# Reordering the attention slot: scores and their maximum first, reciprocal and scaling one slot behind

## The chip, the cores and the metric

The kernel runs on one core of one Trainium2 chip. The metric is device time in microseconds. The engines are named as in the profile: PE is TensorE (matrix products and transposes), PEld its weight loads, DVE is VectorE, ACT is ScalarE, POOL is GpSimd and SP is SyncE, which here only issues DMAs. Each engine takes its own list of instructions from the front, and waits for the others by semaphores.

## The reference

One encoder layer on 512 tokens of width 2048, all in float32. The part that matters here is the attention: eight heads of group A (every query sees all 512 keys) and eight of group B (three dilated windows; they amount to a mask that is added to the scores, since the branches are merged by their softmax denominators).

```python
h = rmsnorm(x, g_mix)
qa, ka, va, qb, kb, vb = split(h @ w_in)
# group A: q, k normalised and rotated, 8 heads of 128, two k/v heads
sc = einsum('bqkgd,bskd->bkgqs', q, k); p = softmax(sc); o = einsum('bkgqs,bskd->bqkgd', p, v)
# group B: the same with the windows (128,1), (512,4), (2048,16), merged by their denominators
x = x + concat(rmsnorm(a), rmsnorm(b)) @ w_out
x = x + (silu(gate) * up) @ w_down          # gate, up = split(rmsnorm(x) @ w_gate_up)
return rmsnorm(x, g_final)
```

## The kernel before

Every float32 product is made from three: each operand is split into a high part (fp32r) and the rest (low part), and `mm3` (L236 to L240) multiplies high by high, high by low and low by high into one bank of PSUM. A split (`split`, L229 and L230) is an ACT copy for the high part and a DVE subtraction for the low part. Weights are split in the same way when they have been loaded (L290 on ACT, L295 on DVE).

The program is written out in the order in which each engine is to run it; no scheduler moves anything. Its main loop goes over units. A unit in the part that matters here multiplies one block of 128 weight rows with the four tiles of 128 tokens, which is twelve products of 512 columns. Ahead of a unit's products, `prepare` issues loads and weight splits of later units; behind them come tasks from a list named `side`, as many as a credit allows (`HEAD_RATE`: 1.42 per unit during the input projection of group B's q and k, 1.9 during the output projection; a slot of group A costs 1.5, one of group B 1.2). So in the input projection less than one slot falls to a unit, and in the output projection now and then two slots follow each other with no unit in between.

The slots are the attention's share of `side`. There are 16 heads of four slots each, and slot s = 4h + i issues, in `head_slot`, the work of several heads at different stages. `score(i)` makes the scores of 128 queries against 512 keys, takes their maximum on DVE (in group B together with the mask, which also moves them from PSUM to the tile p, L572; in group A only the maximum, L568), takes the exponential on ACT with the row sums (L574 and L569), and then, on DVE, the reciprocal of the sums (L576) and the scaling of p by it (L577). Six slots after a head's first scores (`TURN_LAG`), `pt(kb)` transposes the kb-th block of keys of all four p tiles on PE (L583) into one bank, and `split` makes the turned P's high part pTh (ACT) and low part pTl (DVE) from it. Eight slots after (`VALUE_LAG`), `pv(kb)` multiplies V with them. `fin` copies a head's output to the tile oT, stores it to DRAM from ACT's queue (L603), and squares it (L606 or L609) for the later norm. `tq` and `tk` transpose the q and k of a head four and two slots ahead of its first scores.

PSUM has eight banks, which `bank` takes from the front of a queue and `release` puts at its end. A projection chunk holds four of them, a running P·V product one. The tiles named by `slot` share storage that is laid out over the whole program from each tile's first to its last use.

Of the kernel before, what the change touches and what calls it, by code (L numbers as in the profile page):

```python
# [14 lines left out]
AF = mybir.ActivationFunctionType  # L15
# [8 lines left out]
NT = S // P  # L24
# [33 lines left out]
TURN_LAG = 6  # L58
VALUE_LAG = 8
# [8 lines left out]
def encoder_block(ctx, tc, x, g_mix, w_in, g_q_a, g_k_a, g_out_a, g_out_b, w_out, g_ffn,  # L68
                  w_gate_up, w_down, g_final, c_ident, c_mask, c_axial, c_partial, out):
    nc = tc.nc  # L70
# [9 lines left out]
    def nm(base):  # L80
        counter[0] += 1
        return f"{base}_{counter[0]}"

    def slot(base, dtype=F32, shape=(P, 512)):
        return sp.tile(list(shape), dtype, tag="s", name=nm(base))
# [11 lines left out]
    def bank():  # L97
        return banks.popleft()

    def release(*tiles):  # L100
        banks.extend(tiles)
# [3 lines left out]
    def small(n=4):  # L105
        used[0] += n
        assert used[0] <= 512
        return smalls[:, used[0] - n:used[0]]
# [127 lines left out]
    def mm3(dst, a, b, start, stop, chained=False):  # L236
        (ah, al), (bh, bl) = a, b
        nc.tensor.matmul(dst, ah, bh, start=start, stop=False, skip_group_check=chained)  # L238
        nc.tensor.matmul(dst, ah, bl, start=False, stop=False, skip_group_check=chained)  # L239
        nc.tensor.matmul(dst, al, bh, start=False, stop=stop, skip_group_check=chained)  # L240

    def cols(pair, lo, n=P):
        return pair[0][:, lo:lo + n], pair[1][:, lo:lo + n]
# [288 lines left out]
    class Head:  # L532
# [27 lines left out]
        def score(self, t):  # L560
            if t == 0:
                self.negm, self.z, self.rz = small(), small(), small()
            ps = bank()
            mm3(ps, cols(self.q, t * P), self.k, True, True)
            p = slot("p")
            nmx, z, rz = self.negm[:, t:t + 1], self.z[:, t:t + 1], self.rz[:, t:t + 1]
            if self.kind == "A":
                nc.vector.tensor_reduce(nmx, ps, axis=AX.X, op=OP.max, negate=True)  # L568
                nc.scalar.activation(p, ps, AF.Exp, bias=nmx, accum_out=z)  # L569
            else:  # L570
                lo = (NT - 1 - t) * P
                nc.vector.tensor_tensor_reduce(p, ps, mask[:, lo:lo + S], -1.0, 3e38, op0=OP.add, op1=OP.min,  # L572
                                               accum_out=nmx)
                nc.scalar.activation(p, p, AF.Exp, bias=nmx, scale=-1.0, accum_out=z)  # L574
            release(ps)
            nc.vector.reciprocal(rz, z)  # L576
            nc.vector.tensor_scalar(p, p, rz, None, op0=OP.mult)  # L577
            self.p[t] = p

        def pt(self, kb):  # L580
            ps = bank()
# [42 lines left out]
    def head_at(slot):  # L624
        h, i = divmod(slot, NT)
        return (heads[h], i) if 0 <= h < len(heads) else (None, i)

    def head_slot(s):
        head, i = head_at(s - TURN_LAG)
        if head:  # L630
            head.pt(i)
        head, i = head_at(s - VALUE_LAG)
        if head:
            head.pv(i)
            if i == NT - 1:
                head.fin()
        head, i = head_at(s)
        if head:
            head.score(i)
        for lead in ("tq", "tk"):  # L640
            head, i = head_at(s + {"tq": 4, "tk": 2}[lead])
            if head and i == 0:
                getattr(head, lead)()

    def weighed(cost, f):
        f.cost = cost
# [5 lines left out]
    def attention_tasks():  # L652
# [38 lines left out]
        for s in range(2 * NHA * NT + VALUE_LAG + 1):  # L691
            cost = 1.5 if s < NHA * NT else 1.2 if s < 2 * NHA * NT else 0.7
            todo += [weighed(cost, lambda s=s: head_slot(s))] + extra.get(s, [])
# [580 lines left out]
    at = [0.0]  # L1274
# [56 lines left out]
    for n, u in enumerate(units):  # L1331
# [20 lines left out]
        while side and credit >= getattr(side[0], "cost", 1.0):  # L1352
            f = side.popleft()
# [58 lines left out]
```

## Time and profile before

| what | value |
|---|---|
| median of 3 runs | 2008.81 us (2008.07 to 2009.35) |
| profiled execution | 2008.06 us, span 2006.3 us |
| granted TensorE clock, mean | 0.996 |
| PE busy | 1982.6 us, 99% |
| DVE busy | 1565.2 us, 78% |
| ACT busy | 1113.2 us, 55% |
| POOL busy | 129.1 us, 6% |

The profile gives each engine's busy time, the groups of instructions by line with the idle time ahead of them and what ended it, the waits summed by who waited for whom, the chain of work that ended last, and the timeline. The span is the time from the first to the last instruction of the profiled execution. "L583" is line 583 of the kernel; where a helper issues an instruction, its line is the helper's, so the pieces of `split` and `mm3` are told apart by the tiles that they write and read (`b` is a bank of PSUM, `smalls` a column of small per-row values, `arena` a large tile that also holds split weights and activations).

### The profile page before, as it was taken

The numbers are of one execution on the slowest core, as the hardware profiler recorded it, in microseconds if no ns is written. First come the engines' busy times: TensorE is split into PE (matmuls) and PEld (weight loads), VectorE is DVE, ScalarE is ACT, GpSimd is POOL, SyncE is SP. The second block draws the span as 40 slices with busy tenths as digits, with TensorE's granted clock in tenths as the row PEclk, the third lists the DMA queues.
The fourth block names the chain that finished last, engine by engine and source line by source line (L and its number), as shares of the span: only waits on it lengthen the run. The fifth ranks groups of instructions, "written<-read, shape, count | busy, mean of one in ns | idle before, by whom it ended". The sixth has DMA issues, their size and how long they took to land.

```text
span 2006.3 us, 27422 instructions
## 1 busy us (share of the span) xinstructions
PE 1982.6 (99%) x9019; PEld 1632.3 (81%) x9019; DVE 1565.2 (78%) x2786; ACT 1113.2 (55%) x1984; POOL 129.1 (6%) x161
## 2 busy tenths in 40 slices
PE   9999999999999999999999999999999999999997
PEld 7888888887788888888888888888888888788886
DVE  6887876666764688878877878778789887877968
ACT  8655345455544565555555555545545666666655
POOL 0000100000010000000000000000000122111121
PEclk9999999999999999999999999999999999999999
DMA  8576533335244645737647558458367698768765
GB/s 275 179 280 230 178 116 99 106 133 166 91 140 138 210 144 197 268 123 260 233 147 275 196 182 283 152 195 299 122 240 253 194 279 251 191 172 270 195 159 168
DMA packets 231135, 390.61 MB, mean 195 GB/s; under 512 B 21408, under 2 KB 70352, under 8 KB 230864
## 3 DMA queue, kind: packets, MB, share of 16 engines
q1 hardware_dynamic: 204736, 325.87, 48.2%
q0 software_dynamic: 15280, 34.09, 8.2%
q10 hardware_dynamic: 10976, 28.91, 4.1%
q8 instruction: 70, 1.15, 0.2%
q14 instruction: 73, 0.60, 0.1%
HBM read 325.08 MB, written 63.70 MB: 194 GB/s over the span
## 4 chain that ended last, share of the span: by engine, by line
PE 92%; DVE 3%; issue 2%; ACT 2%; DMA 1%; POOL 0%; ACTq 0%; POOLq 0%; DVEq 0%
PE b L238 29%; PE b L239 29%; PE b L240 29%; PE b L583 1%; DVE tw L780 1%; PE b L1084 1%; DVE raw L817 1%; DMA x<-x1d 0%; PE b L1009 0%; PE b L319 0%; PE b L545 0%; DVE pTl L230 0%; DMA oA<-oT 0%; POOL x1d L1156 0%; DMA oB<-oT 0%
## 5 line engine op out<-in xcount | busy, mean ns | idle before, releaser
L238 PE MATMUL b<-tw,arena 128*128 128x512 f32 x2136 | 837.5, 392 | 2.5 <-ACT ev L1155 2.5
L239 PE MATMUL b<-tw,arena 128*128 128x512 f32 x2136 | 831.9, 389 | 0.6 <-DVE tw L780 0.5
L240 PE MATMUL b<-tw,arena 128*128 128x512 f32 x2136 | 832.3, 390 | 0.1
L777 ACT ACTIVATE tw<-raw 128x512 fp32r<-128x512 f32 x924 | 559.1, 628 | 433.3 <-DVE raw L817 282.7
L780 DVE TENSOR_TENSOR tw<-raw,tw 128x512 fp32r<-128x512 f32 x924 | 618.7, 686 | 169.8 <-ACT tw L777 166.6
L238 PEld LDWEIGHTS b<-tw,arena 128*128 128x128 f32 x2136 | 401.0, 188 | 84.9 <-ACT ev L1155 3.6
L240 PEld LDWEIGHTS b<-tw,arena 128*128 128x128 f32 x2136 | 400.9, 188 | 84.8 <-DVE arena L330 0.5
L239 PEld LDWEIGHTS b<-tw,arena 128*128 128x128 f32 x2136 | 401.2, 188 | 83.7 <-DVE tw L780 1.8
L817 DVE TENSOR_TENSOR raw<-raw,raw 128x512 f32<-128x512 f32 x528 | 361.5, 685 | 1.1 <-DMA raw<-in_w_gate_up_dram 0.9
L238 PE MATMUL b<-w,arena 128*128 128x512 f32 x368 | 146.1, 397 | 0.0
L239 PE MATMUL b<-w,arena 128*128 128x512 f32 x368 | 143.6, 390 | 0.7 <-DVE w L295 0.7
L240 PE MATMUL b<-w,arena 128*128 128x512 f32 x368 | 143.8, 391 | 0.0
L1156 POOL DMA_DIRECT2D x1d<-ev x76 | 66.4, 974 | 1147.1 <-ACT ev L1155 1127.2
L239 PEld LDWEIGHTS b<-w,arena 128*128 128x128 f32 x368 | 69.2, 188 | 15.3 <-DVE w L295 1.5
L240 PEld LDWEIGHTS b<-w,arena 128*128 128x128 f32 x368 | 69.1, 188 | 14.9
L777 ACT ACTIVATE tw<-stage 128x512 fp32r<-128x512 f32 x96 | 58.0, 628 | 40.2 <-DVE stage L817 29.4
L238 PEld LDWEIGHTS b<-w,arena 128*128 128x128 f32 x368 | 69.1, 188 | 13.5
L780 DVE TENSOR_TENSOR tw<-stage,tw 128x512 fp32r<-128x512 f32 x96 | 64.0, 686 | 12.2 <-ACT tw L777 12.1
L295 DVE TENSOR_TENSOR w<-raw,w 128x512 fp32r<-128x512 f32 x96 | 64.8, 684 | 6.5 <-ACT w L290 3.5
L230 DVE TENSOR_TENSOR pTl<-b,pTh 128x512 fp32r<-128x512 f32 x64 | 43.9, 687 | 30.8 <-ACT pTh L229 28.1
L290 ACT ACTIVATE w<-raw 128x512 fp32r<-128x512 f32 x96 | 58.2, 622 | 15.6 <-PE b L239 6.8
L357 DVE TENSOR_TENSOR pair<-pair 128x256 f32<-128x256 f32 x120 | 45.5, 421 | 26.2 <-ACT pair L1012 25.1
(193 smaller groups left out, 1749.9 us busy)
## 6 DMA issues: line engine op xcount, KB each, us to landing
raw<-in_w_gate_up_dram SPq DMA_DIRECT2D x616, 256.0 KB, 5.3
raw<-in_w_down_dram SPq DMA_DIRECT2D x176, 256.0 KB, 6.8
stage<-in_w_in_dram SPq DMA_DIRECT2D x112, 256.0 KB, 5.3
forms<-pair SPq DMA_DIRECT2D x22, 896.0 KB, 5.3
x1d<-ev POOLq DMA_DIRECT2D x76, 256.0 KB, 6.8
fr<-forms ACTq DMA_DIRECT2D x35, 512.0 KB, 6.0
raw<-in_w_in_dram SPq DMA_DIRECT2D x64, 256.0 KB, 5.2
raw<-in_w_out_dram SPq DMA_DIRECT2D x32, 512.0 KB, 4.6
```

What stands on the lines that cost most here:

```text
L230: nc.vector.tensor_tensor(lo, src, f32(hi), op=OP.subtract)
L238: nc.tensor.matmul(dst, ah, bh, start=start, stop=False, skip_group_check=chained)
L239: nc.tensor.matmul(dst, ah, bl, start=False, stop=False, skip_group_check=chained)
L240: nc.tensor.matmul(dst, al, bh, start=False, stop=stop, skip_group_check=chained)
L290: nc.scalar.activation(self.w[0], src, AF.Copy)
L295: nc.vector.tensor_tensor(self.w[1], self.src, f32(self.w[0]), op=OP.subtract)
L357: nc.vector.tensor_tensor(out, x, y, op=op)
L583: nc.tensor.transpose(ps[:, t * P:(t + 1) * P], self.p[t][:, kb * P:(kb + 1) * P], ident)
L777: nc.scalar.activation(self.pair[:, 0], self.src, AF.Copy)
L780: nc.vector.tensor_tensor(self.pair[:, 1], self.src, f32(self.pair[:, 0]), op=OP.subtract)
L817: nc.vector.tensor_tensor(t[dst], t[src[0]], t[src[1]], op=OP.add if form == "m6" else OP.subtract)
L1156: nc.gpsimd.dma_start(x1_dram[2 * cb + j, row], e, accum_op=OP.add)
```

## The change

The exponential leaves `score` for a step of its own, `exp`, and the reciprocal with the scaling goes to `norm`. A slot issues, in this order: scores and maximum of slot s; reciprocal and scaling of the scores of slot s-1; transposes and split of P (lag 6); the exponential of slot s; P·V (lag 8) and, at a head's end, `fin`; then `tq` and `tk`. Before, the order was: transposes and split of P, P·V and `fin`, then scores, maximum, exponential, reciprocal and scaling, then `tq` and `tk`. In group A the bank with the scores is released after the exponential, which now stands behind the transposes; in group B it is released after the masked maximum, as that reads it last.

```diff
-            p = slot("p")
-            nmx, z, rz = self.negm[:, t:t + 1], self.z[:, t:t + 1], self.rz[:, t:t + 1]
+            p = self.p[t] = slot("p")
+            nmx = self.negm[:, t:t + 1]
             if self.kind == "A":
                 nc.vector.tensor_reduce(nmx, ps, axis=AX.X, op=OP.max, negate=True)
-                nc.scalar.activation(p, ps, AF.Exp, bias=nmx, accum_out=z)
+                self.raw = ps
             else:
                 lo = (NT - 1 - t) * P
                 nc.vector.tensor_tensor_reduce(p, ps, mask[:, lo:lo + S], -1.0, 3e38, op0=OP.add, op1=OP.min,
                                                accum_out=nmx)
+                release(ps)
+
+        def exp(self, t):
+            p, nmx, z = self.p[t], self.negm[:, t:t + 1], self.z[:, t:t + 1]
+            if self.kind == "A":
+                nc.scalar.activation(p, self.raw, AF.Exp, bias=nmx, accum_out=z)
+                release(self.raw)
+            else:
                 nc.scalar.activation(p, p, AF.Exp, bias=nmx, scale=-1.0, accum_out=z)
-            release(ps)
+
+        def norm(self, t):
+            p, z, rz = self.p[t], self.z[:, t:t + 1], self.rz[:, t:t + 1]
             nc.vector.reciprocal(rz, z)
             nc.vector.tensor_scalar(p, p, rz, None, op0=OP.mult)
-            self.p[t] = p
...
     def head_slot(s):
-        head, i = head_at(s - TURN_LAG)
-        if head:
-            head.pt(i)
-        head, i = head_at(s - VALUE_LAG)
-        if head:
-            head.pv(i)
-            if i == NT - 1:
-                head.fin()
-        head, i = head_at(s)
-        if head:
-            head.score(i)
-        for lead in ("tq", "tk"):
-            head, i = head_at(s + {"tq": 4, "tk": 2}[lead])
-            if head and i == 0:
-                getattr(head, lead)()
+        def at(lag, f, only=None):
+            head, i = head_at(s - lag)
+            if head and (only is None or i == only):
+                f(head, i)
+        at(0, Head.score)
+        at(1, Head.norm)
+        at(TURN_LAG, Head.pt)
+        at(0, Head.exp)
+        at(VALUE_LAG, Head.pv)
+        at(VALUE_LAG, lambda head, i: head.fin(), NT - 1)
+        at(-4, lambda head, i: head.tq(), 0)
+        at(-2, lambda head, i: head.tk(), 0)
```

## The prediction

> **What bounds the kernel now.** I read the page first, then busy time by stretches of the span, then the waits inside the stretch with holes, then the timeline of the largest hole. The head of the page:
>
> ```profile
> span 2006.3 us, 27422 instructions
> PE 1982.6 (99%) x9019; PEld 1632.3 (81%) x9019; DVE 1565.2 (78%) x2786; ACT 1113.2 (55%) x1984; POOL 129.1 (6%) x161
> ```
>
> TensorE is the bound, and it stands idle for only 2006.3 - 1982.6 = 23.7 us. The edit keeps all instructions, so it can win only TensorE's idle time in the attention, and time lost to a lowered clock. Busy time by stretches (time, then busy us of each engine and instruction count, granted clock, DMA), and below them the transposes of P (shortest, median, longest in ns, first and last start), which say where the slots lie:
>
> ```profile
> 240.00:440.00 200.00, 199.97 (x970) 164.72 (x969) 134.96 (x316) 98.09 (x208) 13.24 (x12) 1.00 0.33 106
> 440.00:545.00 105.00, 96.22 (x465) 76.86 (x464) 74.18 (x179) 57.45 (x121) 6.24 (x5) 0.97 0.43 140
> 545.00:590.00 45.00, 45.00 (x225) 36.98 (x224) 29.21 (x59) 24.04 (x48) 6.59 (x5) 1.00 0.43 142
> 474.64:480.43 5.79, 2.90 (x16) 1.82 (x14) 3.76 (x9) 2.91 (x6) 0.00 (x0) 0.92 0.85 291
> 480.43:486.59 6.16, 6.16 (x17) 5.03 (x18) 4.26 (x11) 3.90 (x9) 0.00 (x0) 0.52 0.20 66
> ...
> L583 PE MATMUL b<-fixed,p x256: 270/272/475, 272.4 to 578.1; 128*128 128x128 f32 x128
> ```
>
> Up to 440 us and after 545 us TensorE is full: nothing to win there. In between it lacks 105.00 - 96.22 = 8.8 us. Right behind the largest hole the clock granted over 6.16 us is 0.52, which costs 6.16 x 0.48 = 3.0 us more. The most that the edit can win is thus 8.8 + 3.0 = 11.8 us. Who is waited for between 440 and 545 us (total us, times, longest; the last row is group A's, over the whole span):
>
> ```profile
> PE b L583 <- DVE pTl L230: 4.1, 3, 2.4
> PE b L238 <- DVE pTl L230: 1.7, 3, 0.7
> PE b L238 <- DVE x L963: 1.1, 1, 1.1
> PE b L583 <- DVE qTl L230: 0.7, 1, 0.7
> PE b L239 <- DVE w L295: 0.7, 1, 0.7
> PE b L238 <- ACT acc L606: 0.5, 1, 0.5
> DVE smalls L576 <- ACT p L574: 19.6, 21, 1.6
> DVE pTl L230 <- ACT pTh L229: 7.0, 8, 1.6
> ACT pTh L229 <- DMA oA<-oT: 2.2, 1, 2.2
> ACT pTh L229 <- DMA oB<-oT: 2.0, 1, 2.0
> ...
> DVE smalls L576 <- ACT p L569: 30.0, 32, 2.0
> ```
>
> The six PE rows add up to the 8.8 us, and 8.3 of them end on VectorE. Yet VectorE is busy for 74.18 of 105 us. It is late because it also waits: 19.6 us ahead of the reciprocal L576, in every one of the 21 slots, for ScalarE's exponential. The largest hole shows it (timelines of DVE, then PE):
>
> ```profile
> 474.44 0.68 DVE L230 TENSOR_TENSOR pTl<-b,pTh 128x512 fp32r<-128x512 f32 x1
> 475.04 0.68 DVE L572 CUSTOM_DVE_ANT_0 p<-b,mask 128x512 f32<-128x512 f32 x1
> 475.65 0.08 DVE L572 DVE_READ_ACCUMULATOR2_ANT smalls<- 128x1 f32 x1
> 477.28 0.16 DVE L576 RECIPROCAL smalls<-smalls 128x1 f32<-128x1 f32 x1 [1.55 <-ACT p L574]
> 477.48 0.49 DVE L577 TENSOR_SCALAR p<-p,smalls 128x512 f32<-128x512 f32 x1
> 478.42 0.75 DVE L233 SCALAR_TENSOR_TENSOR arena<-oback,fixed,arena 128x512 fp32r<-128x512 f32 x1 [0.45 <-ACT arena L232]
> 479.08 0.69 DVE L295 TENSOR_TENSOR arena<-raw,arena 128x512 fp32r<-128x512 f32 x1
> 479.69 0.69 DVE L230 TENSOR_TENSOR pTl<-b,pTh 128x512 fp32r<-128x512 f32 x1
> 477.40 0.60 PE L545 MATMUL b<-fixed,qkB 128*128 128x128 f32 x4
> 480.43 1.11 PE L583 MATMUL b<-fixed,p 128*128 128x128 f32 x4 [2.43 <-DVE pTl L230]
> ```
>
> VectorE stands 1.55 us ahead of the reciprocal; behind it queue the scaling, two splits and the pTl that frees the bank into which TensorE wants to transpose next. TensorE's idle of 2.43 us is that queue's lateness.
>
> **The change, part by part.** No instruction is added or removed; the chain in a slot was pTh, pTl, maximum, exponential, reciprocal, scaling, with two hand-overs to ScalarE on VectorE's path.
>
> *Reciprocal and scaling one slot behind.* They now find an exponential finished in the slot before, so the 19.6 us of waits (30.0 us more in group A, where TensorE has no holes) leave VectorE. What VectorE does in a slot, by the start distances and durations above: maximum 0.69, reciprocal 0.20, scaling 0.49, pTl 0.60, together 1.98 us, with 0.61 for a weight's low part per unit. TensorE's side, from the chain of waits, at the full and the lowered clock:
>
> ```profile
> 460.64 0.44 PE b L583 x4
> 461.08 0.23 PE b L238
> 480.43 1.11 PE b L583 x4
> 481.54 0.43 PE b L238
> ```
>
> A slot takes TensorE 6 x 0.23 + 0.44 = 1.82 us, a unit of twelve products 2.76 us. Over the stretch the demand on VectorE is 74.18 us against 105 - 11.8 = 93.2 us of TensorE: 80%. It fits, with 19.0 us spare. The consumer is not hurried by the later scaling: the transposes of a head begin at slot 4h+6, the last scaling now falls in slot 4h+4.
>
> *Scores and maximum first.* The scores move past the four transposes and the P·V products on TensorE, so pTh and pTl start 3 x 0.23 = 0.69 us later in the slot. P·V reads them two slots later, at least 3.6 us of slots away, and that covers it; without the cover it costs 0.69 us per slot. The maximum depends on TensorE alone.
>
> *pTl behind maximum, reciprocal and scaling.* This counts where the next transposes go into the bank that pTl frees. I followed the queue of banks by hand: of eight, a chunk holds four and the P·V product one. In group B, as before, slots 1 and 3 of a head transpose into the bank of the slot before. From one set of transposes to the next lie, in slots without a unit between, P·V 0.69, the q or k transposes 0.44 and scores 0.69: 1.82 us. pTl is done 0.69 + 0.20 + 0.49 - 0.44 + 0.60 = 1.54 us after the transposes. That leaves 0.28 us, so a pair without a unit between stalls when VectorE is later than that, which it is where a q, k or v split (0.6 us each) or rope work lies in between. In group A the bank of the scores is held until the exponential, and pTl's bank passes on in nearly every slot; but there a whole unit lies between (0.69 + 2.76 + 0.69 = 4.1 us against 1.54). I cost that at nothing; with this cover gone it would be the short stalls of group B, 0.5 to 0.7 us each.
>
> *Exponential behind pTh on ScalarE,* as before, but now also ahead of oT, its store and the square at a head's end. These come 0.72 us (the exponential) plus its accumulator read later. They free the P·V bank; the one wait seen on it is 0.5 us (L606). Between a gain of 0.5 us and a loss of 8 x 0.5 = 4 us for eight heads I take 0, because ScalarE is busy 57.45 of 105 us and no longer waits for a late maximum. The stores' issues move by the same time; POOL's sums and SP's loads keep their order.
>
> *Storage of the tiles* is laid out over the whole program, and a new order lays it out anew. The trace can't show how. Rows of the chain for the two waits on it:
>
> ```profile
> 448.33 4.30 DMA oA<-oT
> 533.97 4.10 DMA oB<-oT
> oA<-oT ACTq DMA_DIRECT2D x8, 256.0 KB, 3.1
> oB<-oT ACTq DMA_DIRECT2D x6, 256.0 KB, 4.1
> ```
>
> They held pTh back by 2.2 and 2.0 us and ended in 0.7 (the w row) and 1.2 us of TensorE's idle. Bounds: both vanish (they are in the 11.8), or each store of group B hits VectorE (the last rival). I take one of about 1 us as staying.
>
> *Sum.* The old holes close but for a rest. How many slots have no unit between, from the groups of the same stretch (first products of the units, and the exponentials):
>
> ```profile
> L238 PE MATMUL b<-arena,arena 128*128 128x512 f32 x48 | 19.9, 414 | 1.1 <-DVE x L963 1.1
> L238 PE MATMUL b<-w,arena 128*128 128x512 f32 x22 | 8.9, 404 | 0.0
> L574 ACT ACTIVATE p<-p,smalls 128x512 f32<-128x512 f32 x21 | 15.2, 722 | 30.0 <-DVE smalls L572 30.0
> ```
>
> That is 21 slots to (48 + 22) / 4 = 17 units, so some four pairs have no unit between; at 0.4 us each that is 1.5 us, and with the storage wait 2.5 us. Gain in idle 8.8 - 2.5 = 6.3 us; no hole near 2.4 us remains, so the 3.0 us of clock come too: 9.3 us. The profiled execution took 2008.06 us (span 2006.3 and 1.8 around it), 0.75 below the median of 2008.81; profiled that makes 1998.8, as a median 1999.5 us.
>
> The Trainium skill (TensorE: Matmul & The Clock Gate, "HAM oscillation — how this bites in real kernels") speaks of idle gaps over about 3.4 us as what drops the clock to half. Here the half clock is seen (0.52), but behind a hole of 2.43 us with one of 0.5 us before it; the trace differs in the length. If the dip had another cause and stayed, the gain would be 6.3 us, 2002.5 us; that lies in the range below.
>
> **Rivals.** (1) *VectorE stays the local bound.* For it: splits and rope work come in bunches, and single waits end on qTl, x and w, not on P. Then half the idle stays, 4.4 us, and the dip with it: gain 4.4 us, 2004.4 us. Against it: 80% demand, and the waits that go are twice the holes. (2) *The holes only move.* If TensorE's waits come from the bank turn in pairs of slots and not from the exponential, they come back one slot later: 2008.8 us. For it: the two largest holes are bank waits (L583). Against it: at 480.43 pTl stood behind the reciprocal's wait, in plain sight. (3) *Slower: the tile behind the store.* The tile asked for next after oT's store is now P of the next score, and in group B VectorE writes it ahead of all else in the slot. If it is laid over oT, VectorE stands until the store lands: 4.2 us, less the 1.82 us that TensorE has in hand, is 2.4 us. Six stores of group B make 14.4 us, and a dip 3.0: 2008.8 - 11.8 + 14.4 + 3.0 = 2014.4 us. It decides from four hits on. For it: such waits exist now. Against it: two long ones in 14 stores. The skill (Perfetto Trace Analysis, "Optimization Strategy") reads repeated bubbles as a possible lack of room for the next tile; the two DMA waits above agree with that as far as they go.
>
> **How the numbers follow.** Forecast 58%, its own range 1997.0 (nothing left) to 2002.5 (dip or twice the rest left). Rival 1 16%, rival 2 11%, rival 3 15%. About 0.2% of 2008.8, 4 us, can be told from no change. Faster: the forecast and, at 4.4 us, some two thirds of rival 1, 0.69; slower: rival 3, 0.15; the rest 0.16. The range leaves out rival 3 and the upper half of rival 2: 1996.0 to 2009.0.
>
> **What would show it.** Right: waits of the reciprocal on the exponential near zero, TensorE busy for all but about 2.5 us of the slots' time, granted clock 1.00 throughout them, and the first 440 us unchanged. Rest stalls should be of transposes for pTl, under 0.8 us, in slots 1 and 3 of group B. Wrong: holes as large with VectorE free of ScalarE's waits (rival 2), or VectorE's masked maximum waiting for a DMA of oT (rival 3). The forecast also fails if holes appear in group A, or if the new layout delays loads outside the attention.

## The result and the profile after

The changed kernel takes 1998.41 us (median of 4 runs, 1996.02 to 1999.84), the kernel before on the same chip 2009.01 us: a ratio of 0.9942, 95% interval 0.993 to 0.9955, 10.6 us faster. Run again later beside other kernels it took 1997.49 us, ratio 0.9942 (0.9929 to 0.9954). Its profiled execution took 1999.84 us at a mean granted clock of 0.998. The head of its page:

```profile
span 1998.1 us, 27432 instructions
PE 1980.0 (99%) x9019; PEld 1634.5 (82%) x9019; DVE 1559.6 (78%) x2786; ACT 1109.5 (56%) x1984; POOL 130.1 (7%) x161
```

The engines' instruction counts in the second line are those of before, as an edit of order alone must leave them; TensorE's idle time is 1998.1 - 1980.0 = 18.1 us where it was 23.7. Busy time by stretches of the span (columns as in the prediction), then the stretch behind the largest hole:

```profile
240.00:440.00 200.00, 198.69 (x964) 164.25 (x964) 132.72 (x320) 94.95 (x206) 14.00 (x12) 1.00 0.32 105
440.00:545.00 105.00, 102.73 (x516) 84.65 (x515) 79.96 (x197) 62.45 (x131) 6.21 (x5) 0.98 0.46 148
545.00:590.00 45.00, 45.00 (x221) 37.22 (x220) 25.33 (x50) 19.97 (x41) 6.65 (x5) 1.00 0.41 134
...
481.64:485.00 3.36, 3.36 (x10) 2.88 (x11) 3.06 (x7) 2.51 (x7) 0.00 (x0) 0.50 0.20 32
```

Between 440 and 545 us TensorE's idle fell from 8.8 to 2.3 us, and 516 products start there where 465 did. A new 1.3 us appeared in group A (first row). The clock still drops to half behind the largest hole, but for 3.36 us instead of 6.16. The waits between 440 and 545 us (total us, times, longest):

```profile
ACT pTh L229 <- PE b L592: 27.8, 15, 3.5
DVE p L572 <- PE b L240: 12.8, 10, 2.1
ACT p L582 <- DVE smalls L572: 6.3, 8, 1.5
DVE arena L233 <- ACT arena L232: 4.4, 5, 2.3
...
PE b L238 <- DVE smalls L572: 1.7, 1, 1.7
...
PE b L545 <- ACT sq L618: 0.4, 1, 0.4
PE b L592 <- DVE pTl L230: 0.2, 1, 0.2
```

L586, the reciprocal, waits in no row of the whole stretch: before, it waited 19.6 us. The first two rows are the sign of health: ScalarE and VectorE now wait for TensorE's transposes (L592) and scores (L240), so they are ahead of it. Before, the same stretch read:

```profile
ACT p L574 <- DVE smalls L572: 30.0, 17, 3.2
...
ACT pTh L229 <- PE b L583: 4.6, 4, 1.5
...
DVE p L572 <- PE b L240: 0.9, 2, 0.7
```

There ScalarE's exponential waited 30.0 us for the masked maximum, and little waited for TensorE's transposes and scores (4.6 and 0.9 us). What is left of the largest hole, in the timeline of the changed kernel (start, duration, and in brackets the wait ahead of the instruction and what ended it):

```profile
474.96 0.72 ACT L582 ACTIVATE p<-p,smalls 128x512 f32<-128x512 f32 x1 [1.28 <-DVE smalls L572]
...
475.69 0.58 ACT L609 ACTIVATE oT<-b 128x512 f32<-128x512 f32 x1
476.67 0.60 ACT L615 ACTIVATE acc<-b 128x512 f32<-128x512 f32 x1 [0.40 <-ACT oT L609]
477.16 0.62 ACT L290 ACTIVATE arena<-raw 128x512 fp32r<-128x512 f32 x1
477.68 0.71 ACT L232 ACTIVATE arena<-oback,fixed 128x512 fp32r<-128x512 f32 x1
478.43 0.75 DVE L233 SCALAR_TENSOR_TENSOR arena<-oback,fixed,arena 128x512 fp32r<-128x512 f32 x1 [2.30 <-ACT arena L232]
479.10 0.68 DVE L295 TENSOR_TENSOR arena<-raw,arena 128x512 fp32r<-128x512 f32 x1
479.70 0.68 DVE L572 CUSTOM_DVE_ANT_0 p<-b,mask 128x512 f32<-128x512 f32 x1
480.44 0.50 PE L238 MATMUL b<-kTh,qTh 128*128 128x512 f32 x1 [1.69 <-DVE smalls L572]
```

A head's end (L609, L615) and two splits for units stand in ScalarE's queue; VectorE waits 2.30 us for the second split's high part (L232), makes two low parts, and only then the maximum that frees the bank for TensorE's next scores. Work of other parts comes in a bunch here, and the edit has a share in it: the exponential (first line), which now goes ahead of the head's end on ScalarE, waits 1.28 us for its maximum, and the head's end and both splits stand behind it. In e8_low and e9_low_nolag below, where the head's end goes first, the hole at this place is 1.01 us, though there the square makes two others, of 1.0 and 0.6 us. No run moves the head's end alone.

Where the 8.2 us between the two profiled executions (2008.06 and 1999.84) lie: the kernel reaches the attention (first transposes of k) at 246.4 us instead of 244.4; the attention, up to the first transposes of the output projection's result, takes 390.2 us instead of 399.6; the MLP up to its last gate and up transposes takes the same (956.6 and 956.5); the rest, the down projection, 404.9 instead of 405.8. That is +2.0 - 9.4 + 0.1 - 0.9 = -8.2. The 2.0 us at the start are not the edit's: the same kernel, run again, begins the attention at 244.6. The attention of the two kernels, as one row each:

```profile
244.40:644.00 399.60, 390.79 (x1874) 319.60 (x1873) 259.37 (x578) 198.06 (x408) 25.01 (x20) 0.99 0.37 121
```

```profile
246.40:636.60 390.20, 386.62 (x1874) 319.42 (x1873) 254.28 (x578) 194.57 (x408) 25.47 (x20) 1.00 0.38 124
```

With the same 1874 products TensorE's idle fell from 8.8 to 3.6 us, its busy time from 390.79 to 386.62. Of these 4.2 us the shorter dip (the time at half clock) accounts for 3.0 - 1.7 = 1.3, and the number of holes (10 before, 4 after) for 6 x 0.16 = 1.0: a product's record lasts 0.39 us though the next starts 0.23 us later, so each closed hole gives 0.16 us more than its recorded idle. The other 1.9 us I did not itemise.

### The profile page after: what moved, and what is told of

Same layout as the page of the kernel before. It is cut to its first block, busy times and chain, and to the rows that moved or that the text cites. A ratio compares the mean times of both kernels' runs of the same rounds, so it can differ in the third digit from the quotient of the medians.

```text
span 1998.1 us, 27432 instructions
## 1 busy us (share of the span) xinstructions
PE 1980.0 (99%) x9019; PEld 1634.5 (82%) x9019; DVE 1559.6 (78%) x2786; ACT 1109.5 (56%) x1984; POOL 130.1 (7%) x161
## 5 line engine op out<-in xcount | busy, mean ns | idle before, releaser
L240 PE MATMUL b<-tw,arena 128*128 128x512 f32 x2136 | 833.2, 390 | 0.0
L240 PEld LDWEIGHTS b<-tw,arena 128*128 128x128 f32 x2136 | 401.3, 188 | 83.9
L240 PE MATMUL b<-w,arena 128*128 128x512 f32 x368 | 143.9, 391 | 0.0
L229 ACT ACTIVATE pTh<-b 128x512 fp32r<-128x512 f32 x64 | 38.3, 598 | 117.2 <-PE b L592 109.2
L240 PEld LDWEIGHTS b<-w,arena 128*128 128x128 f32 x368 | 69.1, 188 | 15.1
```

Source lines behind the costliest of these rows:

```text
L229: nc.scalar.activation(hi, src, AF.Copy)
```

## The experiments

All are read by the same three stretches, because a new order also lays out the tiles' storage anew and so moves the down projection by some us. "Attention" and "down" are the stretches just named, in the profiled execution; the ratio is that of the medians to the kernel before on the same chip.

| kernel | order on VectorE, ScalarE, TensorE | median us (runs) | ratio, 95% | attention us (idle) | down us |
|---|---|---|---|---|---|
| before | pTl max norm; pTh exp; transposes first | 2009.01 (4) | | 399.6 (8.8) | 405.8 |
| e1_behind | pTl max norm'; pTh exp; transposes first | 2008.42 (11) | 0.9987 to 1.0005 | 394.8 (6.3) | 410.1 |
| e2_first | max norm pTl; exp pTh; scores first | 2013.26 (11) | 1.0013 to 1.0031 | 399.2 (9.1) | 412.8 |
| e3_expfirst | max norm' pTl; exp pTh; scores first | 2007.4 (11) | 0.9982 to 1.0 | 398.4 (8.5) | 407.1 |
| e9_low_nolag | max pTl norm; pTh exp; transposes first | 1999.53 (5) | 0.9943 to 0.9968 | 390.7 (4.5) | 404.8 |
| e8_low | max pTl norm'; pTh exp; transposes first | 2003.52 (6) | 0.9959 to 0.9982 | 390.7 (4.6) | 409.3 |
| e4_same | max pTl norm; pTh exp; scores first | 2000.7 (5) | 0.9946 to 0.9971 | 387.8 (3.1) | 408.1 |
| after | max norm' pTl; pTh exp; scores first | 1998.41 (4) | 0.993 to 0.9955 | 390.2 (3.6) | 404.9 |
| after_again | as after | 1997.49 (5) | 0.9929 to 0.9954 | 388.1 (3.1) | 405.2 |

In the second column "max" is the maximum, "exp" the exponential, "norm" the reciprocal and the scaling, norm' that of the slot before; pTl and pTh are the halves of the turned P. The repeat shows how far two executions of one kernel lie apart in the attention: 2.1 us, of which 1.7 is the dip that one has and the other hasn't. Differences under that are not read.

**e1_behind: only the distance of a slot.** The old order, with reciprocal and scaling one slot behind.

```diff
-        at(0, Head.score)
-        at(1, Head.norm)
         at(TURN_LAG, Head.pt)
-        at(0, Head.exp)
         at(VALUE_LAG, Head.pv)
         at(VALUE_LAG, lambda head, i: head.fin(), NT - 1)
+        at(0, Head.score)
+        at(0, Head.exp)
+        at(1, Head.norm)
```

> The order of the kernel before (turned P, P·V, scores, maximum, exponential), with the reciprocal and the scaling alone moved one slot behind. Theory (VectorE's wait for the exponential made it late): the reciprocal's waits between 440 and 545 us fall from 19.6 us to under 2, and nearly the whole gain is here: 1996 to 2002 us. Rival (scores and maximum ahead make the gain): 2005 to 2010 us.

Measured 2008.42 us, no change, as the rival said. What the prediction took for the cause was gone from the trace (the reciprocal waits for nothing) and yet TensorE's largest hole stood. Waits of e1_behind between 440 and 545 us, on ScalarE, VectorE and TensorE:

```profile
ACT p L582 <- DVE smalls L572: 27.1, 16, 2.7
DVE pTl L230 <- ACT pTh L229: 9.6, 10, 2.1
...
DVE arena L233 <- ACT arena L232: 5.2, 6, 2.1
DVE kTl L230 <- ACT kTh L229: 5.0, 6, 1.1
DVE qTl L230 <- ACT qTh L229: 4.5, 5, 1.3
...
PE b L592 <- DVE pTl L230: 2.9, 2, 2.4
```

Most of VectorE's wait for ScalarE has moved from the reciprocal to the low parts: they wait 9.6 + 5.2 + 5.0 + 4.5 = 24.3 us. Before, it was 19.6 us ahead of the reciprocal and 7.0 + 2.3 = 9.3 ahead of low parts (pTl and L233), so 15 of the 19.6 us came back. The exponential still waits 27.1 us for the masked maximum (30.0 before), and the high parts that ScalarE makes next stand behind it. The largest hole, in the timelines of ScalarE, VectorE and TensorE:

```profile
475.87 0.60 ACT L615 ACTIVATE acc<-b 128x512 f32<-128x512 f32 x1 [1.84 <-PE b L239]
476.36 0.71 ACT L582 ACTIVATE p<-p,smalls 128x512 f32<-128x512 f32 x1
...
477.59 0.71 ACT L232 ACTIVATE arena<-oback,fixed 128x512 fp32r<-128x512 f32 x1
478.33 0.75 DVE L233 SCALAR_TENSOR_TENSOR arena<-oback,fixed,arena 128x512 fp32r<-128x512 f32 x1 [2.09 <-ACT arena L232]
480.34 1.11 PE L592 MATMUL b<-fixed,p 128*128 128x128 f32 x4 [2.42 <-DVE pTl L230]
```

VectorE now stands 2.09 us ahead of a weight's low part (L233), since the high part for it (L232) is queued on ScalarE behind the exponential, and that behind a head's end whose square (L615) waited 1.84 us for TensorE. The kernel before has the same 1.84 us at this place; the prediction read the wait of the reciprocal there and not what stood in ScalarE's queue ahead of the exponential. The attention gained 4.8 us, of which 2.5 is idle time and about 1.6 a shorter drop of the clock (0.63 over 3.66 us behind the hole, 1.4 us lost where it was 3.0); the down projection lost 4.3 (see e7_before_pt).

**e2_first and e3_expfirst: the exponential ahead of pTh.** Scores, maximum, exponential and scaling all ahead of the turned P (e2), and the changed kernel with the exponential alone moved ahead (e3):

```diff
         at(0, Head.score)
+        at(0, Head.exp)
         at(1, Head.norm)
         at(TURN_LAG, Head.pt)
-        at(0, Head.exp)
```

> Scores, maximum, exponential, reciprocal and scaling all ahead of the turned P, with no slot between. Theory: the reciprocal waits for the exponential again, about 0.9 us in each slot, and pTl now stands behind that wait: no gain, 2005 to 2014 us. Rival (scores and maximum ahead make the gain): 1996 to 2002 us.

> The changed kernel with the exponential ahead of the turned P, so that pTh waits for it on ScalarE. Theory: the reciprocal still finds its exponential done, but pTl is done some 2.7 us behind the scores instead of 2.0, which is 0.4 us too late for the next transposes in slots that follow each other without a unit: 2 to 4 us slower than the changed kernel, 2000 to 2004 us, with holes of transposes for pTl. Rival (the place of the exponential does not matter): as the changed kernel, 1996 to 2000 us.

Measured 2013.26 us, as expected, and 2007.4, more than the 2000 to 2004 expected: with the exponential ahead of pTh nearly all of the gain is gone, with the scaling one slot behind or not. Waits of e3_expfirst between 440 and 545 us:

```profile
ACT p L582 <- DVE smalls L572: 40.7, 19, 4.0
DVE pTl L230 <- ACT pTh L229: 15.6, 20, 0.8
...
PE b L592 <- DVE pTl L230: 2.9, 4, 1.1
...
PE b L238 <- DVE smalls L572: 2.5, 1, 2.5
```

ScalarE waits 40.7 us for the maximum in nearly every slot (19 times), with pTh queued behind it, and VectorE's pTl waits for that pTh 20 times. In the changed kernel the first of these rows is 6.3 us.

**e4_same: no distance, the new order.** The changed kernel with reciprocal and scaling in their own slot, behind the exponential.

```diff
-        at(1, Head.norm)
         at(TURN_LAG, Head.pt)
         at(0, Head.exp)
+        at(0, Head.norm)
```

> The changed kernel with reciprocal and scaling behind the exponential of the same slot: scores, maximum, turned P, exponential, reciprocal, scaling, P·V. Theory: pTl now fills part of VectorE's wait, so the reciprocal waits some 0.3 to 0.5 us in a slot instead of 0.9, and half or more of the gain is kept: 1998 to 2005 us. Rival (only a whole slot of distance helps): 2005 us and more.

Measured 2000.7 us, and the attention 387.8 us is the shortest of all. Its waits in the same window:

```profile
ACT p L582 <- DVE smalls L572: 11.5, 11, 1.9
...
DVE pTl L230 <- ACT pTh L229: 5.6, 13, 0.9
...
DVE smalls L586 <- ACT p L582: 3.2, 11, 0.3
```

The reciprocal of the same slot waits 3.2 us, not 19.6: with the low part between the maximum and the reciprocal the exponential is almost done when VectorE asks for it. The slot's distance isn't needed.

**e8_low and e9_low_nolag: only the maximum ahead of pTl.** TensorE's and ScalarE's orders are those of before; on VectorE alone the low part of the turned P goes behind the maximum. e8 has the distance of a slot, e9 hasn't. The edit of e8 against e1_behind:

```diff
-            self.pTs[kb] = split(ps, "pT")
-            release(ps)
+            hi, lo = self.pTs[kb] = slot("pTh", F32R), slot("pTl", F32R)
+            nc.scalar.activation(hi, ps, AF.Copy)
+            self.turned = ps
+
+        def low(self, kb):
+            hi, lo = self.pTs[kb]
+            nc.vector.tensor_tensor(lo, self.turned, f32(hi), op=OP.subtract)
+            release(self.turned)
...
         at(0, Head.score)
+        at(TURN_LAG, Head.low)
         at(0, Head.exp)
```

> The kernel e1_behind with one more step on VectorE alone: the maximum of the new scores ahead of pTl. TensorE's and ScalarE's orders stay those of the kernel before. New theory (a ring between VectorE and ScalarE: maximum, exponential, next pTh, next pTl, next maximum, closed once in every slot, sets the pace; it opens when the maximum no longer stands behind pTl): 1997 to 2003 us, and VectorE's waits for ScalarE fall from some 24 us to under 12 between 440 and 545 us. Rival (the scores ahead on TensorE make the gain): 2005 to 2010 us.

> The kernel e8_low without the distance of a slot: turned P's high part, P·V, scores, maximum, pTl, exponential, reciprocal, scaling. From the start of the attention (first transposes of k) to the transposes of the output projection's result the profiled executions took 399.6 us before, 394.8 in e1_behind, 390.7 in e8_low. Theory (maximum ahead of pTl opens the ring; the distance of a slot is then worth what VectorE still waits ahead of the reciprocal, about 0.3 us in a slot): 389 to 393 us for this stretch, TensorE idle in it 3 to 6 us. Rival (the distance of a slot is what counts): 396 us and more, idle over 7 us.

Both attentions take 390.7 us. Against the kernel before, from which e9 differs by this alone, that is 8.9 us less: one exchange on one engine's queue, between work that was already there, is worth about what the whole change is. Against e1_behind, from which e8 differs by it alone, it is 4.1 us less, and VectorE's waits for ScalarE come to 6.4 us, as expected, where e1_behind has 24.3. One thing comes with the exchange: the bank of the turned P is now given back behind that of the scores, so the banks are taken in another turn (in both runs TensorE's transposes wait for a maximum, 1.5 us in all, where in the kernel before and in e1_behind they wait for pTl). No run parts the two. Medians 2003.52 (just above the 2003 expected) and 1999.53 us differ by the down projection (409.3 and 404.8). e9_low_nolag's waits:

```profile
ACT p L582 <- DVE smalls L572: 26.2, 17, 3.0
DVE p L572 <- PE b L240: 9.9, 8, 1.8
...
DVE smalls L586 <- ACT p L582: 6.7, 20, 0.8
```

The exponential still waits 26.2 us for the maximum, but now because scores come last on TensorE in the slot (the maximum itself waits for them), and pTh is ahead of it. So this wait's size says little; what is queued behind it counts.

**after_again, e5_ev4: what is left.** The changed kernel once more, and with four buffers of their own for the tiles `evqkB`, whose stores a split waited for:

```diff
-            e = homes.popleft() if name == "kvA" else slot("ev" + name)
+            e = homes.popleft() if name == "kvA" else sp.tile([P, 512], F32, tag="evq", bufs=4, name=nm("ev" + name))
```

> The changed kernel once more, for its spread on this chip and a second trace: 1996 to 2000 us, with the holes at 325 and 480 us as in the first trace; where the clock behind the hole at 480 us stays at 1.00, the time is about 1.7 us shorter.

> The changed kernel with the evacuated q and k of group B in four buffers of their own, so that no tile of the attention is laid over a store of theirs that still runs. Theory (the rest of the holes begins with VectorE's waits on these stores, 3.6 us ahead of pTl at 325 us and 1.4 us ahead of kTl at 472 us): both waits vanish, the hole of 1.3 us goes and that of 1.7 us shrinks with its clock dip: 1993 to 1997 us. Rival (the hole at 480 us comes from the bunch of splits there): only the 1.3 us go, 1996 to 1999 us.

TensorE's waits over the attention (230 to 640 us) in after_again:

```profile
PE b L592 <- DVE pTl L230: 1.5, 2, 1.2
PE b L238 <- DVE smalls L572: 1.3, 1, 1.3
PE b L545 <- ACT sq L618: 0.3, 1, 0.3
```

The time is as expected, the holes are the same, and the one for the masked maximum is shorter. The first row's 1.2 us lies in group A, as in the first run of the changed kernel (timeline):

```profile
325.25 0.69 DVE L230 TENSOR_TENSOR pTl<-b,pTh 128x512 fp32r<-128x512 f32 x1 [3.63 <-DMA qkB<-evqkB]
326.00 0.66 PE L592 MATMUL b<-fixed,p 128*128 128x128 f32 x4 [1.31 <-DVE pTl L230]
```

There pTl is laid over a tile whose store hasn't landed. e5_ev4 takes these waits away (DMA waits of VectorE and ScalarE in the attention 8.1 us, then 2.2) and doesn't win: the attention takes 390.8 us, the hole for the maximum stays,

```profile
479.25 0.50 PE L238 MATMUL b<-kTh,qTh 128*128 128x512 f32 x1 [2.47 <-DVE smalls L572]
```

and the down projection takes 409.3; the whole 2004.32 us (0.9964 to 0.9982), slower than the change and than both forecasts. This doesn't settle what the stores cost at 480 us: in the new layout the square at the head's end (L615) waits 3.3 us for TensorE's L240, and VectorE 5.2 us for the split behind it, waits that the changed kernel doesn't have.

**e7_before_pt: the layout alone.** The kernel before with six buffers of their own for pTh and pTl: its order is untouched, the storage isn't.

```diff
-            hi, lo = slot(name + "h", F32R), slot(name + "l", F32R)
+            hi, lo = (sp.tile([P, 512], F32R, tag="pT", bufs=6, name=nm(name + n)) if name == "pT" else slot(name + n, F32R)
+                      for n in "hl")
```

> The kernel before with six buffers of their own for the two halves of the turned P, so that neither is laid over a store of oT. Theory (the waits on stores are a small part of the holes): pTh's two waits on DMA vanish with the holes of 0.7 and 1.2 us, the rest stays: 2005.5 to 2008 us. Rival (the new layout of storage, not the order, makes the gain): 2002 us or less.

2010.94 us (1.0002 to 1.002), above both forecasts. The two holes of 0.7 and 1.2 us went, as expected, and a new one of 2.1 us came, because one masked maximum now waits 2.8 us for a DMA of x (9.2 us idle in all). The largest, 2.48 us for pTl, stands, though the square at the head's end no longer waits 1.84 us there. So it needs neither the stores of oA and oB nor this wait of the square. The down projection grew from 405.8 to 408.9 us by layout alone. What it looks like there, in the waits of SyncE's queue 30 to 90 us into it, first of the changed kernel, then of e1_behind:

```profile
SPq L267 <- DVE tw L786: 10.8, 13, 3.2
```

```profile
SPq L267 <- DVE tw L786: 22.7, 9, 19.7
```

One load of w_down waits 19.7 us for storage that a VectorE split still holds (19.2 in e7_before_pt). TensorE then does 162 products in the 40 us from 1676 us of e1_behind, where the changed kernel does 176 at the same place:

```profile
1676.00:1716.00 40.00, 37.72 (x162) 29.63 (x161) 29.77 (x45) 22.25 (x36) 6.75 (x8) 1.00 0.73 191
```

A wait of 19 to 20 us stands in e1, e2, e4, e5, e7, e8 and e11, which have 408.1 to 412.8 us in the down projection; the kernels without it (before, after and its repeat, e3, e9, e10) have 404.8 to 407.1. It goes with the layout, which I saw and didn't control.

**e10_cost and e11_same_cost: other weights for the slots.** The planner's cost of a slot of group B from 1.2 to 1.35 in the changed kernel and in e4_same, to spread the units otherwise.

```diff
-            cost = 1.5 if s < NHA * NT else 1.2 if s < 2 * NHA * NT else 0.7
+            cost = 1.5 if s < NHA * NT else 1.35 if s < 2 * NHA * NT else 0.7
```

> The changed kernel with a slot of group B weighed 1.35 instead of 1.2, so that fewer slots follow each other without a unit between. Theory (the hole left at 480 us is a bunch of slots and splits): it falls from 1.3 to 1.7 us to under 1 us, and the stretch from k's transposes to those of the output projection's result from 388 to 390 us to 386 to 388 us; in all 1994 to 1998 us. Rival (the bunch of splits alone makes the hole, or the attention now ends too late for the output projection): no gain, 1997 us and more.

> The kernel e4_same (reciprocal and scaling behind the exponential of the same slot) with the same weight of 1.35. Theory: as e10_cost in the attention, 386 to 388 us for the stretch, since the distance of a slot is worth next to nothing once maximum and pTh go first; in all 1996 to 2001 us, by whether storage in the down projection is laid out as in e4_same (408 us from the last transposes of the gate and up products to the end) or as in the changed kernel (405 us).

2000.12 us (0.9943 to 0.9968) and 2007.26 (0.998 to 0.9998), with attentions of 391.0 and 394.3 us where 386 to 388 were expected. In e10 the hole isn't gone but lies at 489 us, 1.75 us long. In e11 one pTl waits 4.2 us for a store, and TensorE's hole behind it is 2.0 us. No version was shown to beat the changed kernel.

## Why the prediction was right, and where it wasn't

The forecast, 1999.5 us, lies 1.1 us above the median. Its size came out because the cap of 11.8 us and the rest of some 2.5 us were read from TensorE's own holes, which don't depend on the cause. That it came so near is partly luck: in the attention idle time gave 5.2 us for the 6.3 forecast and the clock 1.3 for 3.0, and 2.9 us of shorter busy time, which the sum doesn't have, made up for them. The cause was half right.

**The step that failed** is "reciprocal and scaling one slot behind" as the carrier, with "scores and maximum first" at nothing. The prediction saw VectorE's 19.6 us ahead of the reciprocal and took them for the source of the lateness. e1_behind removes just that wait: the attention gains 4.8 us of the 9.4, the largest hole stays, and the whole time with it. e4_same and e9_low_nolag keep the reciprocal in its slot and have the gain. In a slot VectorE needs pTh from ScalarE for its pTl, and ScalarE needs the maximum from VectorE for its exponential. In the old order VectorE made pTl first, so the two hand-overs stood in a row: pTh 0.60, pTl 0.69, maximum 0.68, exponential 0.72, together 2.7 us, and ScalarE's next high part could not start before the exponential. With the exponential ahead of pTh it is the same ring read from the other end: 0.68 + 0.72 + 0.60 + 0.69 = 2.7 us. A slot without a unit takes TensorE 1.82 us. Only if each engine first does what hangs on TensorE alone, the maximum on VectorE and pTh on ScalarE, do the two run side by side. (The fourth pair, pTl first and the exponential first, would wait for itself.) This ring is an explanation worked out from durations; no run measures it, and as the 21 slots of 105 us lie 5 us apart on average it can press only where slots follow each other. The orders are what the runs show. The attention's times, with and without the slot's distance:

| VectorE first | ScalarE first | own slot | one slot behind |
|---|---|---|---|
| pTl | pTh | 399.6 (before) | 394.8 (e1) |
| maximum | exponential | 399.2 (e2) | 398.4 (e3) |
| maximum | pTh | 390.7 (e9), 387.8 (e4) | 390.7 (e8), 390.2 and 388.1 (the change) |

TensorE's own waits part the groups more sharply. Its holes for pTl in group B add up to 5.8 us before, 4.5 in e1, 6.3 in e2 and 5.3 in e3, but to 0.2 in the change and to none in e4, e8 and e9. What stays in every run of the table is a hole near 480 us of 1.0 to 2.5 us, which ends on pTl before and in e1 and on a masked maximum in the others. Outside the table e11, of the third row, took 394.3 us, 2.0 of them a hole from a store. The cleanest pair is e3 and the change, which differ in ScalarE's order alone (and in layout): 8.2 to 10.3 us. VectorE's exchange was only run together with another turn of the banks.

So "the maximum depends on TensorE alone" was written down as a remark, and was half of the lever, pTh ahead of the exponential the other half. The distance gave 4.8 us in the old order and 0.8 with the exponential first. With maximum and pTh first it gave nothing that stands out: none from e9 to e8, none from e4 to the change, and 3.3 us from e11 to e10, most of it e11's store. The scores ahead on TensorE gave at most 2.9 us (e9 to e4), near the spread of a repeat.

**The other steps.**
- *Holes closed but for 2.5 us:* 3.6 and 3.1 us were left in the attention, 2.3 of the 3.6 between 440 and 545 us. The place was wrong: not short stalls of transposes for pTl (0.2 us in all there) but one of scores for the masked maximum, 1.69 and 1.31 us, at a bunch of splits and a head's end. (The units in its count of pairs are 70 / 4 = 17.5 and not 17, so its 1.5 us of stalls should be 1.4.)
- *Group A at nothing:* one hole of 1.3 us, from a store and not from the bank that the prediction followed. The storage wait of about 1 us was thus foreseen in kind and missed in place.
- *Exponential ahead of oT and the square at 0:* the transposes of q waited 0.4 us for the square, once. The larger cost was not foreseen: where the exponential has to wait for its maximum (1.28 us ahead of the hole at 480 us), the head's end waits with it. How much of that hole it makes is open.
- *The clock:* 3.0 us were to come back; 1.3 came in the first run, all in the repeat.
- *Rivals:* VectorE as a local bound and holes that only move would have left half of the old idle or all of it, and neither did; in e1_behind, with the distance alone, 6.3 of the 8.8 us were left. P behind oT's store does occur (a masked maximum waited 1.8 us for oB in e9_low_nolag), not in the changed kernel, and never four times.
- *Loads outside the attention:* the condition that the forecast named holds for seven of the variants (2 to 7 us more in the down projection than before), and the change's own layout escaped it.

Open: why the start of the kernel differs by about 2 us between executions (the chip runs the same instructions there); what would close the hole at 480 us (the head's end ahead of the exponential is the untried order); the 1.9 us of TensorE's busy time that no row names.

## What to carry to other kernels

Where two in-order engines hand work to each other, find on each queue the instruction that needs only the bound engine and put it ahead of the one that needs the partner; a wait that is merely moved off one instruction comes back on the next while the ring stays closed. Test an order by turning one pair at a time, on one engine, as here one exchange on VectorE, with the turn of banks that goes with it, was worth about the whole change. Compare variants by stage, since an order that wins 9 us in its own stage can lose 4 us in another through the storage that moves with it.

## What the hardware showed

The half clock does not follow from a hole's length alone. In the changed kernel 0.50 was granted over 3.36 us behind a hole of 1.69 us and one of 0.23 us 1.2 us later; in the same execution a hole of 1.66 us in the down projection has 1.00 behind it, as does the hole of 1.31 us of the repeat:

```profile
1719.12 0.51 PE L238 MATMUL b<-tw,arena 128*128 128x512 f32 x1 [1.66 <-ACT ev L1161]
```

```profile
1720.32:1723.12 2.80, 2.80 (x14) 2.28 (x13) 2.63 (x4) 1.84 (x3) 0.88 (x2) 1.00 0.96 203
```

Two holes of nearly one length differ in the same way: behind 2.37 us in e2_first (one of 0.65 us follows 2.2 us later) the clock is 0.50 from 482 to 485 us, behind 2.31 us in e4_same it is 1.00 from 479 to 488 us.

The Trainium skill (TensorE: Matmul & The Clock Gate, "HAM oscillation — how this bites in real kernels") puts the drop behind idle gaps of more than about 3.4 us; here it came behind a hole of 1.69 us, half of that. What else decides it, these runs don't show.
